# Weight sums in DRAM as half pieces on two queues, and the last product of a layer by block of tokens, in a two-layer streaming encoder

## The chip, the cores and the metric

The kernel runs on one core of one Trainium2 chip. The metric is the device time of one execution in microseconds (us). The core has TensorE (PE) for matmuls, whose results go to banks of PSUM; VectorE (DVE), ScalarE (ACT) and GpSimd (POOL) for elementwise work; and SyncE (SP), which here only issues DMAs. [...] Each engine works through its own instructions in order.

## The reference

One inference step over 1024 prompt tokens and 64 tokens of a running stream, all in float32, model width 1024. Layer 0 is a Mamba-2 (SSD) mixer and a SwiGLU feed-forward network (FFN), layer 1 a chunk-band attention with a learned relative bias and an FFN. Every sub-layer has a norm before and after it:

```python
for layer in range(DEPTH):
    if layer < N_A:            # layer 0
        mp = ssd_mixer(rmsnorm(xp, nw[0]), h0, c0, *params)
    else:                      # layer 1
        kp, vp = shared_kv(xp, kv_norm_w, w_kv)
        mp = prompt_band_attention(rmsnorm(xp, nw[0]) @ attn_w_q, kp, vp, attn_rel_bias) @ attn_w_o
    xp = xp + rmsnorm(mp, nw[1])
    xp = xp + rmsnorm(swiglu(rmsnorm(xp, nw[2]), ffn_w_in[layer], ffn_w_out[layer]), nw[3])

def swiglu(u, w_in, w_out):    # hidden width 2816
    g, up = split(u @ w_in, 2)
    return (silu(g) * up) @ w_out
```

The sample tokens go through the same with their own states and caches; outputs are also the new SSD states, convolution rows and the keys and values.

## The kernel before

Activations lie transposed, features on the 128 partitions and the 1088 tokens along the free axis. Every float32 operand is split into a rounded part (hi, made by ACT) and the rest (lo, by DVE), and each product is three matmuls. Tokens are cut in two ways: three slices `SL` of 384, 384 and 320 tokens (s = 0, 1, 2) for the mixer's and the attention's projections, and four quarters `QS` of 256, 256, 288 and 288 (q = 0 to 3) for the rest; blocks b = 0 (q0, q1, 512 tokens) and b = 1 (q2, q3, 576 tokens) are the halves of the FFN.

PE's order is the order in which the program is written out. The program keeps a model clock (`Stream`): side work (norms, splits, the scan's steps, loads) are generator tasks, which yield `(cost, delay, condition)`; a task goes on when the model clock has passed its delay and its condition holds, and what it issues then stands at that place. `st.wait_for` turns the model clock forward until something is there. The other engines' orders come from a scheduler with priorities (`tc.high_priority`). `Ring` objects count tiles: a task that needs tiles of a full ring waits.

The stages, with the times of the profile:

- *Scan* (to about 650 us). 18 groups of two (the last of three) weight tiles of `w_in`, each applied to slices 0, 1, 2: six products ("units") a group. A product ends in one of two PSUM banks named mm; DVE empties it (L798: zs or craw). Beside it `ssd_task` runs for every head pair and slice: it loads a table row MT broadcast over the partitions from DRAM (L922, on SP's queue), DVE takes the column's part off (L931), ACT exponentiates, and PE multiplies. The convolution on ACT starts at L836.
- *Weight sums* (`weight_sums`, L594 to L617). The FFN's second matrix w_f2 is applied by Winograd's form of a 2x2 block product with seven products P1 to P7 instead of eight. Four of them take sums and differences of the matrix's quarters, made once in DRAM: the tensors wsum of each layer, for eight tiles of rows in four groups of two. Each group has five steps: a copy (L608, SP), a sum onto it (L609, POOL), two copies (L610, SP), a sum (L611, POOL), a sum (L612, POOL). The sums of both layers are issued in the scan, three steps ahead of each group from the fifth on.
- *FFN of layer 0* (`back`): first matrix, plain for six pairs and by seven products for the rest, then the second matrix by seven products in the order P1, P6, P7, P5, P4, P2, P3 (`PROD2`); each for four groups g of output rows with 11 tiles of hidden features in two weight parts. `gate2` (L1636 on) puts the products together. After P4 the quarters q1 and q2 are whole, after P3 q0 and q3.
- *Ends.* For a whole quarter, `end(q)` loads the residual stream (delay `EP_W`), computes the norm with `rb_steps` (a transpose of the sums of squares, nst L522; a chain of small DVE steps that makes the reciprocal root nr, L533 to L546; then, `ER_W` later, a broadcast nbp, L552) and applies it (L1566, L1567). `end_slice(s)` splits slice s of the result for the attention (ACT L1591, DVE L1592), sums its squares and, `EQ_W` later, has the next norm's factor made. Slice 0 needs q0 and q1, slice 1 q1 and q2, slice 2 q2 and q3.
- *Attention* (about 1591 to 2100). For each of eight head pairs j a key, value and query product per slice, nine units a pair; between them score, softmax and value steps per block of 128 queries. It begins with values and keys of slice 1, then of slice 0.
- *Output projection and FFN of layer 1*, where P3 already runs first for block 0 and then for block 1.

Weights go through `Weights`: a load on SP into ring raw, a split into ring hl (ACT L363, DVE L364). A pair of w_f1 tiles also has its sum made by a DMA sum on POOL (`aq` in `advance`, L286).

Of the kernel before, what the change touches and what calls it, by code (L numbers as in the profile page):

```python
# [2 lines left out]

# [10 lines left out]
ALU = mybir.AluOpType  # L14
# [36 lines left out]
TB_W, TB_V = 1.0, 10.0  # L51
ES = 0.5, 0.5, 0.4, 0.0
OS = 1.9, 1.4
EP_W, ER_W, EQ_W = ((1.5, 9.4, 12.0, 1.5), (4.0, 9.4, 12.0, 0.0)), (4.0, 8.9, 8.9, 4.0), (5.0, 8.0)

HIP = 3000
BYP = 0, 0, 800, 800
# [178 lines left out]
class Weights:  # L236
# [38 lines left out]
    def advance(self):  # L275
        moved = True
        while moved:
            moved = False
            while self.tq and self.tt.free():
                it = self.tq.pop(0)  # L280
                it["T"] = self.tt.get()
                self.loaded = self.nc.sync.dma_start(it["T"].rearrange("p (e k) -> p e k", e=2), it["two"][0])
                if self.behind is not None:
                    self.tc.add_manual_dep(self.loaded.ins, self.behind.ins.name, ORDER, reason="place in the order")
                self.aq.append((self.clock() + ACC_W, it))
            while self.aq and self.aq[0][0] <= self.clock():  # L286
                it = self.aq.pop(0)[1]
                self.nc.gpsimd.dma_start(it["T"], it["two"][1], accum_op=ALU.add)
                it["added"] = True
            while self.lq and any(r.free() for r in self.raws):  # L290
                self.load()
            if self.sq and len(self.sq[0]["raw"]) == len(self.sq[0]["src"]):
                it = self.sq[0]
                moved = self.plain(it) if len(it["src"]) == 1 else self.pair(it)
# [105 lines left out]
def hybrid_kernel(  # L400
# [188 lines left out]
            UC.put(c)  # L589


    last_g = [None]

    def weight_sums(layer):  # L594

        w2, z, n = w_f2[layer], wsm_[layer], HF * P

        def sp(x):
            tc.add_manual_dep(x.ins, W.loaded.ins.name, ORDER, reason="place in the order")

        def pool(x):
            tc.add_manual_dep(x.ins, last_g[0].ins.name, ORDER, reason="place in the order")

        steps = []
        for g in range(4):
            a, b, to = w2[2 * g], w2[2 * g + 1], z[:, g]
            steps.append((
                lambda g=g, to=to: sp(nc.sync.dma_start(to[:, 2:4, :], w2[2 * g:2 * g + 2, :, :n].rearrange("e p k -> p e k"))),  # L608
                lambda b=b, to=to: pool(G.dma_start(to[:, 2:4, :], b.rearrange("p (e k) -> p e k", e=2), accum_op=ALU.add, max_dma_last_dim=4 * n)),  # L609
                lambda a=a, to=to: (sp(nc.sync.dma_start(to[:, 0, :], to[:, 3, :])), sp(nc.sync.dma_start(to[:, 1, :], a[:, n:]))),  # L610
                lambda a=a, to=to: pool(G.dma_start(to[:, 0, :], a[:, :n], accum_op=ALU.add)),  # L611
                lambda to=to: pool(G.dma_start(to[:, 1, :], to[:, 0, :], accum_op=ALU.add)),  # L612
            ))
        for f in range(5 + 3):
            for g in range(4):
                if 0 <= f - g < 5:
                    yield steps[g][f - g]  # L617

    order = []
    for g in range(NG):  # L620
# [94 lines left out]
    with ExitStack() as es:  # L715
# [92 lines left out]
        class Conv:  # L808
# [5 lines left out]
            def __call__(self, s, ps_):  # L814
                ct = self.ct
                dst = self.dst[s] = sb2.tile([P, 384], F32, tag=self.tag, bufs=self.bufs, name=self.tag)
                raw = sb2.tile([P, 390], F32, tag="craw", bufs=4, name="craw")
                if s == 0:
                    G.memset(raw[:, 0:3], 0.0)
                else:  # L820
                    G.tensor_copy(raw[:, 0:3], self.prev[:, 0:3])
                if s < 2:
                    w_ = 384
                    scaled(raw[:, 3:387], ps_, s, 0, 384)
                    self.prev = sb2.tile([P, 4], F32, tag="halo", bufs=5, name="halo")
                    last_g[0] = G.tensor_copy(self.prev[:, 0:3], raw[:, 384:387])
                else:
                    w_ = 323
                    G.tensor_copy(raw[:, 259:262], scs[:, ct, :])
                    scaled(raw[:, 3:259], ps_, s, 0, 256)  # L830
                    scaled(raw[:, 262:326], ps_, s, 256, 64)
                    G.tensor_copy(cst[:, ct, 0:3], raw[:, 256:259])
                    G.tensor_copy(cst[:, ct, 3:6], raw[:, 323:326])

                cw = C_CW + ct * 4
                A.activation(dst[:, :w_], raw[:, 0:w_], AF.Identity, bias=col(C_CB + ct), scale=col(cw))  # L836
                for k in range(1, 4):
                    V.scalar_tensor_tensor(
                        dst[:, :w_], raw[:, k:k + w_], col(cw + k), dst[:, :w_], op0=ALU.mult, op1=ALU.add
                    )  # L840
                if s < 2:
                    A.activation(dst[:, :384], dst[:, :384], AF.Silu)
                else:
                    A.activation(dst[:, 0:256], dst[:, :256], AF.Silu)
                    A.activation(dst[:, 256:320], dst[:, 259:323], AF.Silu)
                    A.activation(dst[:, 320:384], ident[:, 0:64], AF.Copy, scale=0.0)
# [307 lines left out]
            pend[s] = [dps] * (s < 2) + box  # L1154
        finish(2)
        side[0] = pyy
        staged = chain_of(weight_sums(0), weight_sums(1))
        for i, grp in enumerate(order):
            for _ in range(3 if i > 3 else 0):
                next(staged, lambda: None)()  # L1160
            ws = [W.get() for _ in grp]
            ev = [evac_of(*f) for f in grp]
            if len(grp) < 3:
                seq = [(i, s) for s in range(NSL) for i in range(len(grp))]
                if grp is order[0]:

                    seq = [(0, 0), (0, 1), (1, 0), (1, 1), (1, 2), (0, 2)]
            else:
                seq = [(0, 0), (1, 0), (0, 1), (0, 2), (2, 0), (1, 1), (2, 1), (1, 2), (2, 2)]
            for i, s in seq:  # L1170
                kd_, jj_ = grp[i]
                q = 3 * jj_ + s
                if kd_ == "x":
                    st.wait_for(lambda: so["C"] > q - 5)
                elif kd_ == "z":
                    st.wait_for(lambda: so["D"] > q - 3)
                elif kd_ == "C" and q >= 5:
                    g_, s_ = divmod(q - 5, 3)
                    st.wait_for(lambda: so["C"] > 3 * (4 * g_ + 3) + s_)
                unit(ws[i], u[s], SL[s][1], lambda p_: ev[i](s, p_))  # L1180
                if s == 2:
                    W.put()
        nc.sync.dma_start(cst_o, cst)
# [141 lines left out]

    SEVEN = (P1, (0, 0), None), (P6, None, 0), (P7, None, 3), (P5, None, 2), (P4, None, 1), (P2, (1, 0), None), (P3, (1, 1), None)

    PROD2 = [[(*x, bs) for x in SEVEN for bs in (((0,), (1,)) if lay and x[0] == P3 else ((0, 1),))] for lay in range(2)]

    ACT2 = {P1: 4, P6: 2, P2: 5, P7: 0, P5: 1, P4: 6, P3: 3}  # L1330

# [89 lines left out]
    def back(layer, start, cpost, xsrc, xmid, cpre, cpost2, xout, rb_out, done2):  # L1421
# [3 lines left out]
        with ExitStack() as es:  # L1425
# [230 lines left out]
            def gate2(p_, g, ps, b):  # L1656
# [24 lines left out]
                if p_ == P2:  # L1681
                    add_sq(ssq[q0], a, n, g == 0)
                elif p_ == P5:
                    add_sq(ssq[q1], d, n, g == 0)
                elif p_ == P4:
                    add_sq(ssq[q1], c, n, False)
                elif p_ == P3 and b and g == 3 and rb_out is None:

                    more[0] = ssum_start(n)
                    A.activation(more[0][:, :n], b_, AF.Square)  # L1690
                elif p_ == P3:
                    add_sq(ssq[q0], b_, n, False)

            for p_, _, _, bs in PROD2[layer]:
                for g in range(4):
# [28 lines left out]
                if p_ in (P4, P3):  # L1724
                    for b in bs:
                        q = ((1, 2) if p_ == P4 else (0, 3))[b]
                        st.spawn(end(q, yq[q], ssq[q], more[0] if q == 3 else None))
                    if rb_out is not None:
                        for s in (1,) if p_ == P4 else (0, 2):
                            st.spawn(end_slice(s))  # L1730
            W.pri = 0
            assert RX.live == 0
# [39 lines left out]
    with ExitStack() as es:  # L1772
# [30 lines left out]
        def load_bias(j):  # L1803

            bias = []
            for e in range(2):
                bt = late["sb3"].tile([P, WIN], F32, tag="bias", bufs=3, name="bias")
                nc.sync.dma_start(bt, bass.AP(rbrow.tensor, (2 * j + e) * 768, [[1, P], [1, WIN]]))
                G.memset(bt[0:64, 0:64], NEG)
                G.memset(bt[64:128, 576:640], NEG)  # L1810
                bias.append(bt)
            kqv[j]["bias"] = bias

        def evk(j):
            d = kqv[j]

            def f(s, p_):
# [8 lines left out]
                        G.memset(Kd[:, T:].bitcast(F32), 0.0)  # L1826
                for e, Kd in enumerate(d["Kt"]):
                    hi, lo = Kd[H2[e], 384 * s:384 * s + n], Kd[H2[1 - e], 384 * s:384 * s + n]
                    A.copy(hi, kf[H2[e], :n])
                    V.tensor_tensor(lo, kf[H2[e], :n], hi, op=ALU.subtract)  # L1830
                d["K"].add(s)
                if s:
# [239 lines left out]
        st.wait_for(lambda: cur["A"] >= 3)  # L2072
        units(wq, 0, evq, (2,))
        W.put()
        for j in range(1, 8):
            if j > 1:
                load_pair(j)
# [9 lines left out]
            while left:  # L2087
# [12 lines left out]
                if (s, i) == (2, 0):  # L2100
                    st.spawn(side_task(j))
                units(ws[i], j, evs[i], (s,))
                if s == 2:
                    W.put()
                if j == 7 and i == 2:
# [153 lines left out]
```

## Time and profile before

| | us |
|---|---|
| median of three runs | 2953.83 (2951.97 to 2958.01) |
| profiled execution, its time | 2944.86 |
| profiled execution, its span | 2943.2 |
| PE busy | 2858.4 |
| DVE busy | 2131.8 |
| ACT busy | 1424.9 |
| POOL busy | 605.3 |

The span runs from the first to the last instruction of the profiled execution. A matmul's busy time is modelled, so a stretch in which PE is busy throughout can still be one in which it runs at a lower clock; the clock that was granted stands beside the busy times. In the lines below, `A <- B` after a wait means that A's engine stood idle until B was done; `DMA x<-y` is the landing of a transfer. A row that begins with a time is one instruction: start, duration, engine, line, operation, tiles.

### The profile page before, as it was taken

The page shows a single profiled execution, that of the slowest core. Times are in us where ns is not written, and L with a number is a line of the kernel's source. Part 1 is how long each engine was busy: PE and PEld are TensorE (multiplying, and loading weights), DVE is VectorE, ACT ScalarE, POOL GpSimd, SP SyncE. Part 2 cuts the span into 40 slices and gives each one's busy share as a digit, 9 for nine tenths or more (in the row PEclk, how much of TensorE's full clock was granted, in tenths as well). Part 3 has the DMA queues.
Part 4 walks back from the last instruction along what each step waited for, and adds up shares of the span by engine and source line. Part 5 has one row for each costly group of instructions (what it writes and reads, how often), then busy time and mean ns, then how long its engine had stood idle before and what let it go on. Part 6 is the DMA issues. An engine that isn't in the chain of part 4 may idle for free. (4 is left out here: it accounts for less than half of the span.)

```text
span 2943.2 us, 58213 instructions
## 1 busy us (share of the span) xinstructions
PE 2858.4 (97%) x22094; PEld 2810.2 (95%) x22094; DVE 2131.8 (72%) x4834; ACT 1424.9 (48%) x2616; POOL 605.3 (21%) x880
## 2 busy tenths in 40 slices
PE   8999998999999999999999899999999999999999
PEld 8998898999998999999998899999999999999998
DVE  7987786886767665676559877877768766567567
ACT  6655545554554333344345556656565333334343
POOL 1334334340220222221022000000031122221011
PEclk9999999999999999999999999999999999999999
DMA  4439677654647656577655222222368555667666
GB/s 137 129 132 240 179 206 205 182 162 140 191 143 195 160 142 161 139 213 224 191 173 164 89 65 89 77 72 76 100 202 230 144 146 151 161 188 222 194 197 193
DMA packets 261673, 471.30 MB, mean 160 GB/s; under 512 B 26256, under 2 KB 162672, under 8 KB 261392
## 3 DMA queue, kind: packets, MB, share of 16 engines
q1 hardware_dynamic: 241584, 400.40, 42.0%
q0 software_dynamic: 19808, 67.19, 13.3%
q8 instruction: 173, 2.83, 0.4%
q14 instruction: 108, 0.88, 0.1%
HBM read 381.90 MB, written 127.26 MB: 173 GB/s over the span
## 5 line engine op out<-in xcount | busy, mean ns | idle before, releaser
L489 PE MATMUL mm<-r,hl 128*128 128x384 f32 (+2 forms) x1704 | 571.4, 335 | 25.2 <-DVE zs L798 12.4
L490 PE MATMUL mm<-r,hl 128*128 128x384 f32 (+2 forms) x1704 | 552.4, 324 | 2.4 <-DVE r L1592 2.4
L491 PE MATMUL mm<-r,hl 128*128 128x384 f32 (+2 forms) x1704 | 552.1, 324 | 1.4 <-DVE hl L364 0.7
L489 PEld LDWEIGHTS mm<-r,hl 128*128 128x128 f32 x1704 | 324.1, 190 | 31.6 <-DVE zs L798 12.6
L1379 PE MATMUL px<-r,hl 128*128 128x288 f32 (+1 forms) x1184 | 348.8, 295 | 0.0
L490 PEld LDWEIGHTS mm<-r,hl 128*128 128x128 f32 x1704 | 324.2, 190 | 3.3 <-DVE r L1592 3.0
L491 PEld LDWEIGHTS mm<-r,hl 128*128 128x128 f32 x1704 | 323.3, 190 | 2.0 <-DVE hl L364 1.1
L1380 PE MATMUL px<-r,hl 128*128 128x288 f32 x1056 | 313.3, 297 | 4.6 <-DVE hl L364 4.5
L1378 PE MATMUL px<-r,hl 128*128 128x288 f32 x1056 | 311.6, 295 | 0.0
L364 DVE TENSOR_TENSOR hl<-raw,hl 128x1024 fp32r<-128x1024 f32 (+2 forms) x171 | 195.1, 1141 | 92.9 <-ACT hl L363 92.3
L1714 PE MATMUL po<-r,hl 128*128 128x288 f32 (+1 forms) x856 | 246.7, 288 | 0.0
L1715 PE MATMUL po<-r,hl 128*128 128x288 f32 (+1 forms) x856 | 246.7, 288 | 0.0
L1716 PE MATMUL po<-r,hl 128*128 128x288 f32 (+1 forms) x856 | 246.6, 288 | 0.0
L1379 PEld LDWEIGHTS px<-r,hl 128*128 128x128 f32 x1184 | 223.7, 189 | 0.0
L363 ACT CAST hl<-raw 128x1024 fp32r<-128x1024 f32 (+2 forms) x171 | 165.7, 970 | 110.2 <-PE po L1716 41.4
L1378 PE MATMUL px<-rx,hl 128*128 128x256 f32 x768 | 213.8, 278 | 1.6 <-DVE u L1393 1.6
L1380 PE MATMUL px<-rx,hl 128*128 128x256 f32 x768 | 213.9, 279 | 0.3 <-DVE hl L364 0.3
L1380 PEld LDWEIGHTS px<-r,hl 128*128 128x128 f32 x1056 | 200.1, 189 | 5.4 <-DVE hl L364 5.3
L1378 PEld LDWEIGHTS px<-r,hl 128*128 128x128 f32 x1056 | 200.2, 190 | 0.0
L1379 PE MATMUL px<-rx,hl 128*128 128x256 f32 x640 | 178.3, 279 | 0.0
L1714 PEld LDWEIGHTS po<-r,hl 128*128 128x128 f32 x856 | 161.5, 189 | 0.0
L1716 PEld LDWEIGHTS po<-r,hl 128*128 128x128 f32 x856 | 160.9, 188 | 0.3 <-DVE hl L364 0.3
(385 smaller groups left out, 8019.2 us busy)
## 6 DMA issues: line engine op xcount, KB each, us to landing
raw<-in_w_f_dram SPq DMA_DIRECT2D x64, 512.0 KB, 4.9
tt<-in_w_f_dram SPq DMA_DIRECT2D x44, 512.0 KB, 4.1
tt<-in_w_f_dram POOLq DMA_DIRECT2D x44, 512.0 KB, 6.6
raw<-in_w_in_dram SPq DMA_DIRECT2D x40, 512.0 KB, 4.4
MT<-ascr SPq DMA_DIRECT2D x48, 384.0 KB, 4.9
raw<-in_w_so_dram SPq DMA_DIRECT2D x32, 512.0 KB, 3.8
r<-hscr SPq DMA_DIRECT2D x56, 288.0 KB, 3.9
wsum<-in_w_f_dram SPq DMA_DIRECT2D x8, 1408.0 KB, 10.1
```

Of the source, the lines that this page charges most:

```text
L363: self.nc.scalar.copy(h, v)
L364: (eng or self.eng or self.nc.vector).tensor_tensor(lo, v, h, op=ALU.subtract)
L489: PE.matmul(ps[:, :n], h_, xh, start=(first and i == 0), stop=False)
L490: PE.matmul(ps[:, :n], h_, xl, start=False, stop=False)
L491: PE.matmul(ps[:, :n], l_, xh, start=False, stop=(last and i == nk - 1))
L1378: PE.matmul(ps, wh, ah[:, k, :], start=(k == 0), stop=False)
L1379: PE.matmul(ps, wh, al[:, k, :], start=False, stop=False)
L1380: PE.matmul(ps, wl, ah[:, k, :], start=False, stop=(k == 3))
L1714: PE.matmul(ps, wh, xh, start=(k0 > 0 and i == ks[0]), stop=False)
L1715: PE.matmul(ps, wh, xl, start=False, stop=False)
L1716: PE.matmul(ps, wl, xh, start=False, stop=(k0 == 0 and i == ks[-1]))
```

## The change

Five edits are in the diff:

1. The steps of a weight sum are cut into half pieces (`c = n // 2` columns): eight pieces a layer, of six steps each. Copies are issued from ACT's stream, behind the last convolution or key copy named so far (`last_a`), sums from POOL's as before. Three pieces are under way at a time, each doing one step in turn.
2. Layer 0's sums are issued in the scan, one step after each product of slices 0 and 1 from the second group on; layer 1's in the attention, one step after each unit from pair 1 on.
3. P3 of layer 0 is done for block 0 and then for block 1, as layer 1's already is; the end of q0 and slice 0 are put in after the first, the end of q3 and slice 2 after the second. Its weights are loaded and split once for each.
4. Delays are other: `EP_W` of layer 0 for q1 and q2, `ER_W` of q1 and q2 in both layers, `EQ_W` of slices 0 and 1. The squares of P3's results get a high priority.
5. The DMA sum of a pair of w_f1 tiles is issued only when a pair is next to be split.

```diff
-EP_W, ER_W, EQ_W = ((1.5, 9.4, 12.0, 1.5), (4.0, 9.4, 12.0, 0.0)), (4.0, 8.9, 8.9, 4.0), (5.0, 8.0)
+EP_W, ER_W, EQ_W = ((1.5, 3.0, 6.0, 1.5), (4.0, 9.4, 12.0, 0.0)), (4.0, 5.0, 5.0, 4.0), (12.0, 12.0)
...
-            while self.aq and self.aq[0][0] <= self.clock():
+            while self.aq and self.aq[0][0] <= self.clock() and 'two' in self.sq[0]:
...
-        steps = []
-        for g in range(4):
-            a, b, to = w2[2 * g], w2[2 * g + 1], z[:, g]
-            steps.append((
-                lambda g=g, to=to: sp(nc.sync.dma_start(to[:, 2:4, :], w2[2 * g:2 * g + 2, :, :n].rearrange("e p k -> p e k"))),
-                lambda b=b, to=to: pool(G.dma_start(to[:, 2:4, :], b.rearrange("p (e k) -> p e k", e=2), accum_op=ALU.add, max_dma_last_dim=4 * n)),
-                lambda a=a, to=to: (sp(nc.sync.dma_start(to[:, 0, :], to[:, 3, :])), sp(nc.sync.dma_start(to[:, 1, :], a[:, n:]))),
-                lambda a=a, to=to: pool(G.dma_start(to[:, 0, :], a[:, :n], accum_op=ALU.add)),
-                lambda to=to: pool(G.dma_start(to[:, 1, :], to[:, 0, :], accum_op=ALU.add)),
-            ))
-        for f in range(5 + 3):
-            for g in range(4):
-                if 0 <= f - g < 5:
-                    yield steps[g][f - g]
+        c = n // 2
+        def copy(to, x):
+            behind(A.dma_start(to, x), last_a)
+        def add(to, x):
+            behind(G.dma_start(to, x, accum_op=ALU.add), last_g)
+        def steps(g, o):
+            a, b, to = w2[2 * g], w2[2 * g + 1], z[:, g, :, o:o + c]
+            yield lambda: copy(to[:, 2:4, :], w2[2 * g:2 * g + 2, :, o:o + c].rearrange("e p k -> p e k"))
+            yield lambda: add(to[:, 2:4, :], b.rearrange("p (e k) -> p e k", e=2)[:, :, o:o + c])
+            yield lambda: copy(to[:, 0, :], to[:, 3, :])
+            yield lambda: copy(to[:, 1, :], a[:, n + o:n + o + c])
+            yield lambda: add(to[:, 0, :], a[:, o:o + c])
+            yield lambda: add(to[:, 1, :], to[:, 0, :])
+        pieces = [steps(g, o) for g in range(4) for o in (0, c)]
+        live = []
+        while pieces or live:
+            while pieces and len(live) < 3:
+                live.append(pieces.pop(0))
+            for p_ in list(live):
+                f = next(p_, None)
+                if f is None:
+                    live.remove(p_)
+                else:
+                    yield f
...
-        staged = chain_of(weight_sums(0), weight_sums(1))
-        for i, grp in enumerate(order):
-            for _ in range(3 if i > 3 else 0):
-                next(staged, lambda: None)()
+        staged = weight_sums(0)
+        for grp in order:
...
                 unit(ws[i], u[s], SL[s][1], lambda p_: ev[i](s, p_))
+                if s < 2 and grp is not order[0]:
+                    next(staged, lambda: None)()
...
-    PROD2 = [[(*x, bs) for x in SEVEN for bs in (((0,), (1,)) if lay and x[0] == P3 else ((0, 1),))] for lay in range(2)]
+    PROD2 = [[(*x, bs) for x in SEVEN for bs in (((0,), (1,)) if x[0] == P3 else ((0, 1),))] for lay in range(2)]
...
                 elif p_ == P3:
-                    add_sq(ssq[q0], b_, n, False)
+                    with tc.high_priority(HIP):
+                        add_sq(ssq[q0], b_, n, False)
...
-                        for s in (1,) if p_ == P4 else (0, 2):
+                        for s in (1,) if p_ == P4 else (0,) if bs == (0,) else (2,):
                             st.spawn(end_slice(s))
...
+        staged = weight_sums(1)
         for j in range(1, 8):
...
                 units(ws[i], j, evs[i], (s,))
+                next(staged, lambda: None)()
```

More of the change, by code (lines that the diff above doesn't have):

```diff
@@ L1 @@
 from contextlib import ExitStack
-from itertools import chain as chain_of
 import concourse.bass as bass
@@ L589, in drop_u @@
             UC.put(c)
-    last_g = [None]
+    last_g, last_a = [None], [None]
     def weight_sums(layer):
         w2, z, n = w_f2[layer], wsm_[layer], HF * P
[L598 to L602, printed above, removed]
-        steps = []
-        for g in range(4):
-            a, b, to = w2[2 * g], w2[2 * g + 1], z[:, g]
-            steps.append((
-                lambda g=g, to=to: sp(nc.sync.dma_start(to[:, 2:4, :], w2[2 * g:2 * g + 2, :, :n].rearrange("e p k -> p e k"))),
-                lambda b=b, to=to: pool(G.dma_start(to[:, 2:4, :], b.rearrange("p (e k) -> p e k", e=2), accum_op=ALU.add, max_dma_last_dim=4 * n)),
-                lambda a=a, to=to: (sp(nc.sync.dma_start(to[:, 0, :], to[:, 3, :])), sp(nc.sync.dma_start(to[:, 1, :], a[:, n:]))),
-                lambda a=a, to=to: pool(G.dma_start(to[:, 0, :], a[:, :n], accum_op=ALU.add)),
-                lambda to=to: pool(G.dma_start(to[:, 1, :], to[:, 0, :], accum_op=ALU.add)),
-            ))
-        for f in range(5 + 3):
-            for g in range(4):
-                if 0 <= f - g < 5:
-                    yield steps[g][f - g]
@@ new lines, in weight_sums, with behind @@
+        c = n // 2
+        def behind(x, last):
+            tc.add_manual_dep(x.ins, last[0].ins.name, ORDER, reason="place in the order")
+        def copy(to, x):
[10 more added lines that the diff above has]
+            yield lambda: add(to[:, 1, :], to[:, 0, :])
@@ L835, in __call__ @@
                 cw = C_CW + ct * 4
-                A.activation(dst[:, :w_], raw[:, 0:w_], AF.Identity, bias=col(C_CB + ct), scale=col(cw))
+                last_a[0] = A.activation(dst[:, :w_], raw[:, 0:w_], AF.Identity, bias=col(C_CB + ct), scale=col(cw))
                 for k in range(1, 4):
@@ L1809, in load_bias @@
                 G.memset(bt[0:64, 0:64], NEG)
-                G.memset(bt[64:128, 576:640], NEG)
+                last_g[0] = G.memset(bt[64:128, 576:640], NEG)
                 bias.append(bt)
@@ L1828, in f @@
                     hi, lo = Kd[H2[e], 384 * s:384 * s + n], Kd[H2[1 - e], 384 * s:384 * s + n]
-                    A.copy(hi, kf[H2[e], :n])
+                    last_a[0] = A.copy(hi, kf[H2[e], :n])
                     V.tensor_tensor(lo, kf[H2[e], :n], hi, op=ALU.subtract)
```

## The prediction

> **What bounds the kernel now.** I read the page first (parts 1 and 2), then the busy time by stage, then who PE waited for inside the two stages that the change touches, and last the landing times of the small transfers there.
>
> ```profile
> span 2943.2 us, 58213 instructions
> PE 2858.4 (97%) x22094; PEld 2810.2 (95%) x22094; DVE 2131.8 (72%) x4834; ACT 1424.9 (48%) x2616; POOL 605.3 (21%) x880
> ```
>
> TensorE is the bound over nearly the whole span, so a change can only win what PE loses: 2943.2 - 2858.4 = 85 us of idle time, and what it runs at a lower clock. Where that lies, by stage (columns: PE, PEld, DVE, ACT, POOL busy, granted clock, DMA share, GB/s):
>
> ```profile
> 100.00:209.00 109.00, 108.80 (x778) 106.04 (x777) 98.87 (x244) 65.45 (x99) 47.51 (x73) 1.00 0.37 119
> 209.00:500.00 291.00, 269.21 (x1874) 259.85 (x1874) 217.93 (x559) 146.97 (x217) 114.34 (x178) 0.99 0.76 207
> 500.00:620.00 120.00, 120.00 (x838) 118.19 (x837) 100.91 (x263) 65.07 (x97) 50.34 (x80) 1.00 0.74 205
> 1500.00:1560.00 60.00, 60.00 (x486) 60.00 (x486) 38.76 (x81) 26.03 (x51) 12.54 (x13) 1.00 0.58 177
> 1560.00:1591.00 31.00, 29.79 (x240) 29.53 (x240) 28.16 (x73) 18.03 (x44) 10.04 (x12) 1.00 0.50 159
> 1591.00:1660.00 69.00, 55.77 (x304) 52.52 (x303) 58.99 (x196) 41.59 (x114) 2.13 (x10) 0.93 0.39 122
> 1660.00:2084.00 424.00, 417.57 (x3355) 402.74 (x3353) 329.46 (x1029) 251.79 (x619) 11.32 (x73) 1.00 0.25 76
> ```
>
> Two stages hold it. In the scan, 209 to 500 us, PE idles 291.00 - 269.21 = 21.8 us and 1% of clock costs 2.7 more: **24.5 us**. Just before, without weight sums, it idles 0.2. At the step from layer 0 to attention, 1591 to 1660, it idles 69 - 55.77 = 13.2 us and runs at 0.93, 0.07 x 55.8 = 3.9: **17.1 us**. The attention, 424 us, has ScalarE at 59%, GpSimd nearly empty and DMA at a quarter.
>
> The scan's waits, PE's and then VectorE's (209 to 500: total, times, longest):
>
> ```profile
> PE mm L489 <- DVE zs L798: 12.2, 7, 7.0
> PE mm L489 <- DVE craw L798: 7.3, 6, 2.6
> DVE MT L931 <- DMA MT<-ascr: 35.4, 12, 9.5
> ```
>
> PE waits for VectorE to empty a product's bank (L798), and VectorE, which works in order, stands before L931 until the row table MT has come from DRAM. The landing of MT, from issue, in the windows 100 to 209, 209 to 500 and 500 to 640:
>
> ```profile
> DMA to landing us min/median/max: 3.6/4.3/4.8
> ...
> DMA to landing us min/median/max: 4.0/6.8/15.0
> ...
> DMA to landing us min/median/max: 3.6/4.6/5.5
> ```
>
> And the worst case, one row per engine, as it happened:
>
> ```profile
> 433.68 0.61 SPq L608 DMA_DIRECT2D wsum<-in_w_f_dram  x1
> 434.38 0.56 SPq L610 DMA_DIRECT2D wsum<-wsum  x1
> 435.00 0.59 SPq L610 DMA_DIRECT2D wsum<-in_w_f_dram  x1
> 444.44 1.17 POOL L609 DMA_DIRECT2D wsum<-in_w_f_dram  x1
> 444.75 1.85 SPq L922 DMA_DIRECT2D MT<-ascr  x2
> 458.93 1.20 DVE L931 TENSOR_SCALAR MT<-MT,nac 128x128 f32<-128x128 f32 x6 [9.53 <-DMA MT<-ascr]
> 460.65 0.64 PE L489 MATMUL mm<-r,hl 128*128 128x320 f32 x1 [7.01 <-DVE zs L798]
> ```
>
> Three sum copies on SP's queue and a sum on POOL's stand about the two MT loads; VectorE waits 9.5 us and PE 7.0. At an equal total rate (205 GB/s, 500 to 620) PE lost nothing, so what hurts is a burst that meets an MT load, not the mean rate.
>
> At the step to attention PE waits (1591 to 1660):
>
> ```profile
> PE nbp L552 <- DVE nr L546: 4.3, 1, 4.3
> PE mm L489 <- DVE vt L1876: 3.9, 1, 3.9
> PE mm L490 <- DVE r L1592: 2.4, 2, 1.6
> PE mm L489 <- DVE kf L1822: 1.2, 1, 1.2
> ```
>
> All four are VectorE being late: it is busy 58.99 of 69 us with the ends of q0 and q3, the splits of slices 0 and 2, and the first keys and values at once.
>
> **The change part by part.**
>
> *Weight sums in the scan.* The sums now run as 1408 KB and 704 KB transfers:
>
> ```profile
> wsum<-in_w_f_dram SPq DMA_DIRECT2D x8, 1408.0 KB, 10.1
> wsum<-wsum SPq DMA_DIRECT2D x8, 704.0 KB, 6.6
> ```
>
> Per group of rows that is 2 x 1408 + 4 x 704 = 5632 KB, per layer 22.5 MB; before, two layers within 209 to 620, 110 GB/s. After, one layer here: 48 steps at four steps a group, 12 of the scan's 18 groups of about 30 us (an estimate: they fill the windows from 100 on to some 650 us), 63 GB/s, each transfer half as large, no three steps at once, and no sum copy on the queue that carries MT, only on ACT's and POOL's. What remains of 24.5 us: nothing, if it is as from 500 to 620; 12, if the loss goes with the bytes. I take 6, nearer to nothing, because the 63 GB/s over the scan's own 119 are below those 205. **Gain 18.5** (12 to 24.5). SP loses its 24 copy issues. ACT gains 3 x 8 = 24 at 0.59 us (the last L610 row, of a like size), 14 us in 360, of which it is free for half (146.97 busy of 291). POOL's sum issues stay 24. ACT is in order, though: behind a copy that waits for a sum to land stand the convolution's activations (rival 3).
>
> *Weight sums in attention.* Another 22.5 MB, 24 ACT issues (14 us) and 24 POOL issues (at most 1.17 us each, the L609 row of twice the size: 28 us), spread over 48 of 59 products, about 345 us: 76 + 65 = 141 GB/s. ACT has 424 - 251.79 = 172 us free and POOL over 400. Behind a POOL sum that waits stand the paddings of queries and values, behind an ACT copy the exponentials and P copies, for which PE waits. Bounds: 0 (the 100 to 209 row: 119 GB/s, idle 0.2) and 12 (what bytes alone leave in the scan). **Cost 3**, nearer to the quiet row as to its rate.
>
> *P3 of layer 0 by block.* PE does the same matmuls in another order. The eight half rows of weights are loaded and split twice:
>
> ```profile
> L364 DVE TENSOR_TENSOR hl<-rx,hl 128x768 fp32r<-128x768 f32 x13 | 12.4, 956 | 16.6 <-ACT hl L363 16.5
> L364 DVE TENSOR_TENSOR hl<-rx,hl 128x640 fp32r<-128x640 f32 x14 | 11.7, 835 | 2.2 <-ACT hl L363 2.2
> L363 ACT CAST hl<-rx 128x768 fp32r<-128x768 f32 x13 | 10.8, 833 | 15.3 <-PE po L1716 12.6 <-issue 2.7
> ```
>
> 4 x 0.96 + 4 x 0.84 = 7.2 us more of VectorE, some 6 of ACT, and 2.8 MB. For it the end of q0 and slice 0 start at half of P3, near 1575, instead of at 1591. They cost VectorE, after 1591 now:
>
> ```profile
> L1566 DVE SCALAR_TENSOR_TENSOR y<-y,pcs,rb 128x256 f32<-128x256 f32 x8 | 3.5, 481 | 0.3 <-ACT rb L555 0.3
> L1567 DVE TENSOR_TENSOR y<-y,r 128x256 f32<-128x256 f32 x8 | 3.2, 420 | 0.0
> L1592 DVE TENSOR_TENSOR r<-y,r 128x256 fp32r<-128x256 f32 x8 | 2.9, 420 | 0.0
> ```
>
> 3.5 + 3.2 + 2.9 = 9.6 us leave the crowded stretch, and with slice 0's squares some 12. But P3's own stretch has only 31 - 28.16 = 2.8 us of VectorE free. Room comes from the shorter waits (EP_W, ER_W): the end of q2 and slice 1 move from there into 1500 to 1560, where 21 us are free. With 7.2 + 12 coming in and 8 to 13 going out (an end and a slice, by the same rows, with their squares), P3 is still overfull by 3 to 8 us; the gates and weight splits go first there, so that much runs on past 1591, where PE has three products on slice 1 to do (72 matmuls, some 10 us at the scan row's 269.21 / 1874 each) before it needs slice 0. Late next: the bcast of slice 0, since EQ_W is now 12 us, and the first value weights, whose turn comes later as P3 eats weights twice as fast. I leave 7 of 17.1: **gain 10** (2 to 15).
>
> *Shorter ER_W (8.9 to 5.0), both layers.* For q2 the root's chain on VectorE is slow, as q1's end runs between its steps:
>
> ```profile
> 1549.25 0.49 PE L522 MATMUL nst<-ident,ssum 128*128 128x128 f32 x3
> 1556.34 0.71 DVE L546 SCALAR_TENSOR_TENSOR nr<-nv 128x3 f32<-128x3 f32 x1
> 1559.37 0.49 PE L552 MATMUL nbp<-ident,nr 128*128 128x128 f32 x3
> ```
>
> From nst to the root's end 7.8 us, to nbp 10.1; 3.9 less is 6.2, so PE would stand 1.6 us. Layer 1 has the same chain with the same wait: as much again. **Cost 3.2** (0, if the earlier place finds VectorE free, to 6, if it finds it twice as late).
>
> *The rest.* The new condition for the second sums of the w_f pairs finds the plain weights already split, since three hl tiles hold them; the last group's pair wait (1.6 us, next row) could move by its own size either way, and I cost it at nothing. The priority of P3's squares reorders 0.4 us pieces on ACT that no PE wait names.
>
> ```profile
> PE px L1378 <- DVE u L1393: 1.6, 1, 1.6
> ```
>
> **Sum.** 18.5 + 10 - 3 - 3.2 = 22. Against the profiled execution (2944.9 us, span 2943.2): 2923. The median of the timed runs is 2953.8, 9 us higher than that execution, so I put it at 2953.8 - 22 = **2932**.
>
> **Rivals.**
> 1. *The queue does not matter, only bytes do.* Then 12 of the scan's loss stay, and attention pays 6: 12.5 + 10 - 6 - 3.2 = 13, 2941. For it: POOL's sums stand about the late MT too, and they stay. Against it: equal rates from 209 to 500 and 500 to 620 with unequal landings. [...]
> 2. *The step to attention is not relieved.* Slice 0 needs room in ring R: of 16 tiles slice 1 holds 6, P3's second block 6 and q0's residual 2, so slice 0 waits for P3's last quarter, and VectorE is overfull. Gain 2 instead of 10: 18.5 + 2 - 3 - 3.2 = 14, 2940.
> 3. *ACT blocks* (slower). One copy of each piece, 16 in all, waits on ACT for a sum to land. On POOL such waits cost now:
>
> ```profile
> POOL wsum L612 <- DMA wsum<-in_w_f_dram: 12.1, 3, 5.5
> POOL wsum L609 <- DMA wsum<-in_w_f_dram: 5.3, 2, 4.3
> ```
>
> About 4 us each when they happen. If PE felt 22 / 16 = 1.4 us of each, nothing would be won; at 2.1 us, 33 us are lost, 11 slower than before: 2965. Against it: a piece's next step comes three products later, 15 us, and transfers of sums land in 6.6 to 10.1 (the rows above).
> 4. *Both gains weak* (1 and 2 together, with some of 3): 2950.
> 5. *Nothing comes back*: 24.5 + 15 = 39, 2915.
>
> **How the numbers follow.** Chances: forecast 0.50 (2922 to 2941 by its own bounds), rival 1 0.15, rival 2 0.12, rival 4 0.08, rival 3 0.08, rival 5 0.07. Within 0.2% (5.9 us, about what a measurement of this kernel can tell from no change) falls rival 4; slower is rival 3; the rest, 0.84, is faster. From 2917 to 2946 leaves out rivals 3 and 4 and half of 5.
>
> **What the profile after would show.** MT landing under 8 us throughout, the L931 wait on MT under 10 us in the scan and PE idle there under 8; the same waits near 18 mean rival 1. After P3, L1592 gone from PE's waits and the clock near 1.00; the waits nr and vt still at 4 mean rival 2. A wait of PE for nr of 1 to 2 us at each q2. ACT's waits for wsum landings near zero; tens of us mean rival 3. New PE idle over 5 us between 1660 and 2084 would make the attention cost wrong.

## The result: slower, because the attention lost more than the scan gained

The changed kernel takes 2967.99 us (median of 7 runs, 2963.68 to 2978.93) against 2951.61 for the kernel before: ratio 1.0069, 95% interval [1.0047, 1.009]. The forecast was 2932, faster. The profiled execution of the changed kernel took 2976.23 us, the second longest of the seven, so sizes read from it lean high; that of the kernel before (2944.86) lies 6.8 us under its median. Below, "before" and "after" are the two kernels. One run of e9_no_sums1 further down (3364.06 us, at a granted clock of 0.777 where its other runs show 0.991 to 0.994) is left out of its median and ratio. The head of after's profile:

```profile
span 2974.5 us, 58336 instructions
PE 2876.8 (97%) x22094; PEld 2828.2 (95%) x22094; DVE 2143.4 (72%) x4842; ACT 1425.4 (48%) x2620; POOL 626.6 (21%) x904
```

PE does the same 22094 matmuls, is busy 18.4 us longer and idles 12.9 us more. To find where, take rows that mark the same work in both traces: the first product of layer 0's second matrix (po, first start) and the score products of the attention (S, first and last start). Before, then after (operation, count, durations in ns, first to last start, shapes):

```profile
L1714 PE MATMUL po<-rx,hl x376: 276/281/369, 1358.9 to 2909.2; 128*128 128x256 f32 x132, 128*128 128x288 f32 x56
L1913 PE MATMUL S<-K,Qh x208: 220/309/499, 1647.1 to 2129.1; 128*128 128x320 f32 x64, 128*128 128x128 f32 x16, 128*128 128x256 f32 x8, 128*128 128x384 f32 x8
```

```profile
L1724 PE MATMUL po<-rx,hl x376: 276/281/377, 1346.9 to 2940.8; 128*128 128x256 f32 x132, 128*128 128x288 f32 x56
L1923 PE MATMUL S<-K,Qh x208: 220/309/637, 1634.1 to 2157.2; 128*128 128x320 f32 x64, 128*128 128x128 f32 x16, 128*128 128x256 f32 x8, 128*128 128x384 f32 x8
```

Up to layer 0's second matrix the change is 12.0 us ahead (1358.9 to 1346.9), at the first score 13.0. Across the attention, first to last score, before takes 482.0 and after 523.1: **41.1 us lost**. What follows adds 3.2. 41.1 + 3.2 - 13.0 = 31.3, the difference of the spans. (Some expectations below count to the end of the last score, 482.3 and 523.4; those of e1_anchor, e2_scan and e4_sp begin later, at the last wait for slice 2's keys, and call the same stretch 447 and 488, some 35 us less.)

The stages of after: the scan in two windows, the step to attention, and the attention from the first score to the last; then the attention of before (columns as in the prediction):

```profile
100.00:209.00 109.00, 105.47 (x757) 102.78 (x754) 89.03 (x237) 59.23 (x88) 46.73 (x71) 0.98 0.63 176
209.00:500.00 291.00, 286.29 (x2000) 279.91 (x1999) 238.89 (x600) 160.91 (x241) 127.40 (x196) 0.99 0.61 158
1584.00:1634.00 50.00, 41.38 (x220) 40.02 (x220) 45.49 (x136) 29.23 (x80) 2.25 (x8) 0.90 0.44 142
1634.00:2158.00 524.00, 489.95 (x3829) 468.43 (x3828) 380.15 (x1175) 290.27 (x712) 34.91 (x103) 0.96 0.43 117
```

```profile
1647.00:2130.00 483.00, 473.16 (x3828) 454.88 (x3827) 378.24 (x1175) 290.99 (x712) 13.31 (x79) 1.00 0.26 79
```

In the attention idle time grew from 9.8 us (483 - 473.16) to 34.1, and the same matmuls took 16.8 us longer (489.95 - 473.16) at a clock of 0.96: 24.2 + 16.8 = 41.0.

### One stall, row by row

How a stall of this kind comes about is told by one boundary between two head pairs in the trace of after (start, duration, engine, line, operation, and in brackets the idle time before it and what ended it):

```profile
1758.14 0.15 POOL L1836 MEMSET K<- 128x64 f32 x1 [45.18 <-PE S L1924]
1762.70 0.14 POOL L1819 MEMSET bias<- 64x64 f32 x1 [3.72 <-DMA bias<-in_rbrow_dram]
1762.90 0.15 POOL L1820 MEMSET bias<- 64x64 f32 x1
1763.17 2.82 POOL L605 DMA_DIRECT2D wsum<-in_w_f_dram  x3
1765.28 1.32 SPq L1801 DMA_DIRECT2D cr<-in_ckT_dram  x2
1773.36 0.48 ACTq L602 DMA_DIRECT2D wsum<-wsum  x1
1773.94 0.51 ACT L1861 CAST Qh<-qf 64x384 fp32r<-64x384 f32 x1 [7.68 <-DMA wsum<-in_w_f_dram]
1774.49 0.55 DVE L1863 TENSOR_TENSOR Ql<-qf,Qh 64x384 fp32r<-64x384 f32 x1 [6.47 <-ACT Qh L1861]
1775.29 0.58 PE L1923 MATMUL S<-K,Qh 128*128 128x256 f32 x1 [4.46 <-DVE pT L1958]
1776.87 0.47 PE L488 MATMUL mm<-r,hl 128*128 128x320 f32 x1
1781.16 0.31 PE L488 MATMUL mm<-r,hl 128*128 128x320 f32 x1
```

- POOL has stood 45.18 us before a padding of the keys (L1836), whose buffer the scores of an earlier pair still read. Then come the paddings of the bias tiles (L1819, L1820).
- The diff makes the second of these, L1820, the instruction behind which a sum is placed (`last_g[0] = G.memset(bt[64:128, 576:640], NEG)`). So sums that the program issued one by one, a product apart, all stand behind paddings that wait for a pair to end, and leave together: three in 2.82 us, with copies on ACT's queue about them. It is the same at every pair: all 24 sums of layer 1 leave within 17 us after one of six such paddings of the keys.
- The loads of the keys' cache (cr, L1801) and the weights go out just behind them, and the DMA engines are full: from 1770 to 1777 the windows show a DMA share of 1.07 and 1.08 and up to 284 GB/s, against 0.43 and 117 over the whole attention. The next copy of a piece (1773.36) waits on ACT for a sum to land, and with it the query's split (7.68 us), DVE (6.47) and PE (4.46).
- PE's next matmuls of 320 columns take 0.47 us instead of 0.31, and start 0.27 us apart instead of 0.145; the granted clock is 1.00 from 1770 to 1774, 0.51 from 1774 to 1781 and 1.00 again from 1781 to 1783. The matmuls are slow for some 5.5 us, so this stall cost more than its 4.46 us of idle time.

The same picture in sums over the attention of after: PE's largest wait (2.1 us in before, so it holds 22.4 of the 24.2 us of new idle time), then ACT's on transfers.

```profile
PE S L1923 <- DVE pT L1958: 24.5, 11, 4.8
...
ACT Ck L1803 <- DMA cr<-in_ckT_dram: 17.4, 7, 5.1
ACT Qh L1861 <- DMA wsum<-in_w_f_dram: 15.7, 2, 8.0
...
ACT sc L1938 <- DMA wsum<-in_w_f_dram: 8.6, 1, 8.6
```

And the wait was there to be read before the change (POOL's waits in the attention of before; L1826 and L1809 are after's L1836 and L1819):

```profile
POOL K L1826 <- PE S L1914: 228.4, 10, 45.2
POOL Qh L1845 <- PE S L1913: 68.9, 8, 12.9
POOL bias L1809 <- DVE mx L1923: 59.8, 4, 49.5
```

Of the "over 400 us free" that the prediction gave POOL, little was so: these three rows alone are 357 of the stage's 483 us. POOL was idle, but standing before instructions that could not run yet.

### The profile page after: what moved, and what is told of

It is laid out like the page before. It is cut to its first block, busy times and chain, and to the rows that moved or that the text cites. A ratio compares the mean times of both kernels' runs of the same rounds, so it can differ in the third digit from the quotient of the medians.

```text
span 2974.5 us, 58336 instructions
## 1 busy us (share of the span) xinstructions
PE 2876.8 (97%) x22094; PEld 2828.2 (95%) x22094; DVE 2143.4 (72%) x4842; ACT 1425.4 (48%) x2620; POOL 626.6 (21%) x904
## 5 line engine op out<-in xcount | busy, mean ns | idle before, releaser
L1416 POOL TENSOR_TENSOR u<-u,c 128x256 f32<-128x256 f32 (+1 forms) x76 | 60.9, 802 | 487.1 <-DVE u L1414 404.0
L1724 PEld LDWEIGHTS po<-r,hl 128*128 128x128 f32 x856 | 162.3, 190 | 0.0
```

The source lines that it names most:

```text
L1416: G.tensor_tensor(x["u3"], x["u3"], x["c22"], op=ALU.mult)
L1724: PE.matmul(ps, wh, xh, start=(k0 > 0 and i == ks[0]), stop=False)
```

## The experiments

Three theories for the attention: the sums bunch because of the instruction they are placed behind ("the anchor", theory A), or ACT is held by its own copies, wherever the sums stand (B), or the bytes and issues of the sums cost it as such (C). Further: what in the scan was worth what, and what P3 by block is worth.

**e1_anchor.** One edit to the changed kernel:

```diff
-                last_g[0] = G.memset(bt[64:128, 576:640], NEG)
+                G.memset(bt[64:128, 576:640], NEG)
```

> Edit: the padding of the bias tiles no longer sets the place that POOL's sums must stand behind; everything else is the changed kernel. The attention lasts 447 us before and 488 after (from the last short wait for slice 2's keys to the last score of pair 7). Theory A (POOL works in order, its sums stand behind paddings that wait for a buffer until a pair is done, then go out in a bunch beside the cache loads of the next pair): the sums are spread, the attention falls to 455 to 470. Theory B (an ACT copy that waits for a sum to land holds ACT, wherever the sums stand): 475 to 488. Theory C (the bytes and the issue time of the sums in the attention cost it): 485 to 490.

Measured: 2934.17 us, ratio 0.9956 [0.9942, 0.9971]. Scores and ACT's wait on the cache in the attention; no row of ACT names a sum's landing any more:

```profile
L1923 PE MATMUL S<-K,Qh x208: 220/309/582, 1625.3 to 2114.5; 128*128 128x320 f32 x64, 128*128 128x128 f32 x16, 128*128 128x256 f32 x8, 128*128 128x384 f32 x8
ACT Ck L1803 <- DMA cr<-in_ckT_dram: 7.2, 5, 4.8
```

And POOL at the corresponding place, where the sums now leave one or two at a time, 3.6 to 15 us apart:

```profile
1718.08 0.83 POOL L605 DMA_DIRECT2D wsum<-in_w_f_dram  x1 [14.51 <-DMA wsum<-wsum]
1732.93 1.81 POOL L605 DMA_DIRECT2D wsum<-in_w_f_dram  x2 [14.02 <-DMA wsum<-wsum]
1736.57 0.81 POOL L605 DMA_DIRECT2D wsum<-wsum  x1 [1.84 <-DMA wsum<-in_w_f_dram]
```

The attention takes 489.2 us instead of 523.1, 33.9 less; the ratios of the two kernels to the one before differ by 0.0113, about 33 us. Theory A asked for 455 to 470 in its own measure, which is 490 to 505 here, so the result is just under its lower end; B and C asked for 510 or more. One assignment in one line decided the sign of the whole change, with the same bytes and the same copies: the anchor's theory holds.

**e4_sp.** The changed kernel, anchor and all, with layer 1's copies on SP's queue instead of ACT's:

```diff
-            behind(A.dma_start(to, x), last_a)
+            if layer:
+                tc.add_manual_dep(nc.sync.dma_start(to, x).ins, W.loaded.ins.name, ORDER, reason="place in the order")
+            else:
+                behind(A.dma_start(to, x), last_a)
```

> Edit: the copies of layer 1's sums in the attention go from SP's stream instead of ACT's; sums stay where they are on POOL; the rest is the changed kernel. Theory B: ACT waits for no sum any more, the attention falls from 488 to 465 or less. Theory A: the bunches stay, ACT still waits for the cache loads, 470 to 488, with the waits for wsum now on SP, where other loads stand behind them. Theory C: 485 to 490.

Measured: 2961.26 us, ratio 1.0051 [1.0036, 1.0067]. Scores, and ACT's wait on the cache:

```profile
L1926 PE MATMUL S<-K,Qh x208: 221/309/686, 1629.1 to 2140.6; 128*128 128x320 f32 x64, 128*128 128x128 f32 x16, 128*128 128x256 f32 x8, 128*128 128x384 f32 x8
ACT Ck L1806 <- DMA cr<-in_ckT_dram: 23.3, 11, 5.3
```

511.5 us, as theory A asks (B asked for 500 or less). With ACT freed of its copies 11.6 of the 41 come back; the other 29.5 stay while the sums go out in bunches, and ACT's wait moves to the cache's rows, which land late (6.3 us at the median, 2.7 in before). The two numbers are no clean shares, because SP now stands before the copies as ACT did: it waits 10.6 us for sums to land, and loads stand behind these copies. Holding ACT is a part of the loss, not its source; how large a part stays open.

**e9_no_sums1.** The changed kernel without layer 1's 24 sums (its last products then work with weights that lack them); its copies stay on ACT:

```diff
-            behind(G.dma_start(to, x, accum_op=ALU.add), last_g)
+            if not layer:
+                behind(G.dma_start(to, x, accum_op=ALU.add), last_g)
```

> As the changed kernel, but layer 1's 24 accumulating transfers (the sums, GpSimd's) are left out and the 24 copies on ScalarE's queue stay at their places, so layer 1's last products use wrong weights. Theory 'the sums released together at a pair's end cost attention its time, the copies only pass it on': attention (first to last score matmul) 482 to 488 us instead of 523.4, no wait of ScalarE for a sum's landing, span 2930 to 2940. Rival 'the 24 copies and their 17 MB on ScalarE's queue cost a good part by themselves': over 495 us.

Measured: 2926.72 us (median of three), ratio 0.9932 [0.9915, 0.995]; the profiled span, 2923.5, lies under the 2930 to 2940 expected.

```profile
L1924 PE MATMUL S<-K,Qh x208: 220/309/496, 1624.2 to 2107.3; 128*128 128x320 f32 x64, 128*128 128x128 f32 x16, 128*128 128x256 f32 x8, 128*128 128x384 f32 x8
```

483.1 us, 1.1 more than before: the copies (8 of 704 KB and 16 of 352 KB, 11.3 MB and not the 17 of the expectation) cost the attention next to nothing when they have no sum to wait for. With e1_anchor (489.2), sums that are spread cost about 6, sums that are bunched 40.

**e1c_spread.** As e1_anchor, with the paddings of bias and keys placed behind the last sum, so that none runs ahead:

```diff
-                last_g[0] = G.memset(bt[64:128, 576:640], NEG)
+                late_set(bt[64:128, 576:640], NEG)     # placed behind the last sum issued
...
-                        G.memset(Kd[:, T:].bitcast(F32), 0.0)
+                        late_set(Kd[:, T:].bitcast(F32), 0.0)
```

> As e1_anchor, but the bias and key paddings on GpSimd are placed behind the last sum issued, so that no sum can run far ahead of its product. Theory 'bunching is gone with the anchor': attention (first to last score matmul) 487 to 492 us as in e1_anchor (489.5), ratio 0.994 to 0.997. Rival 'what is left over before (7 us) is still sums going out together': attention 483 to 486, ratio 0.992 to 0.9945. If the paddings now hold up the pair's first scores, attention is over 495.

Measured: 2937.72 us, ratio 0.9959 [0.9942, 0.9975]; scores from 1627.4 to 2115.4, 488.0. No more to be had there; what the remaining 6 us of the sums are made of stays open.

**e2_scan.** The changed kernel with both layers' sums in the scan, as half pieces on the two queues, one step after every product:

```diff
-        staged = weight_sums(0)
+        staged = chain_of(weight_sums(0), weight_sums(1))
...
-                if s < 2 and grp is not order[0]:
+                if grp is not order[0]:
```

> Edit: layer 1's sums go to the scan as well, behind layer 0's, one step after each product from the second group on; no sums in the attention; the rest is the changed kernel. All theories: the attention is back at 447 us. The scan tells how much of its gain was the halved bytes and how much the half pieces and the other queue: PE idle there was 22 us before and is 8 after. If the bytes count, it is 20 or more again and the kernel ends 5 to 8 us below before for nothing but other effects; if pieces and queues count, 8 to 12, and the kernel ends 10 us below before.

Measured: 2954.18 us, ratio 1.0034 [1.0017, 1.0052]. Its scan by stage, and PE's waits from 100 to 640:

```profile
100.00:209.00 109.00, 100.50 (x723) 98.01 (x723) 86.37 (x229) 54.58 (x82) 51.47 (x75) 0.97 0.69 186
209.00:500.00 291.00, 281.10 (x1961) 273.76 (x1960) 233.41 (x582) 155.55 (x235) 130.83 (x200) 0.99 0.73 189
500.00:640.00 140.00, 132.42 (x915) 129.02 (x915) 111.68 (x279) 70.81 (x109) 56.16 (x92) 0.99 0.68 178
```

```profile
PE mm L489 <- DVE craw L808: 14.5, 8, 8.3
PE mm L489 <- DVE zs L808: 9.3, 6, 3.8
```

It idles 8.5 + 9.9 + 7.6 = 26.0 us in these windows; before idled 0.2 + 21.8 + 0. Smaller pieces and other queues brought nothing back: the loss was spread over the scan, not lowered. The idle time is what the case of the bytes asks. The time is not: both cases put the kernel 5 to 10 us under the one before, and it came out 8 above. A marker of the whole scan, the transposes of xsT (tile xtp) from the first to the last, says the same: 575.7 us here, 569.7 in before, 569.3 in e3_p3, which has before's sums. The attention takes 485.1, 3.1 more than before.

**e7_spqueue.** As e1_anchor, with layer 0's copies on SP's queue, which carries the MT loads (the edit of e4_sp with `not layer` for `layer`).

> As e1_anchor, but layer 0's copies of the scan go out on SP's queue, which carries the MT loads, instead of ACT's; bytes, pieces and places are the same. Prediction's case 'a copy ahead of MT in its own queue is what hurts': MT lands later (over 10 us at worst), scan idle rises from 10 to 14 to 20 us, ratio 0.997 to 1.000. Rival 1 'only bytes matter': scan idle stays at 9 to 12 us, ratio 0.994 to 0.9975, as e1_anchor.

Measured: 2940.43 us, ratio 0.9976 [0.9965, 0.9987]. PE's waits from 100 to 640 in it, and then in e6_sums_only, which ran beside it with the copies on ACT's queue:

```profile
PE mm L488 <- DVE zs L810: 10.0, 4, 5.0
PE mm L488 <- DVE craw L810: 1.9, 2, 1.3
```

```profile
PE mm L488 <- DVE zs L807: 7.3, 4, 2.6
PE mm L488 <- DVE craw L807: 2.6, 2, 1.8
```

11.9 us of waiting against 9.9, within the 9 to 12 that rival 1 asks; the slowest MT took 11.9 us to land, against 8.0, and this is what the prediction's case asks (over 10), as is the ratio. The whole scan, by the transposes of xsT, takes 559.9 us. The eight kernels that share its sums, pieces and places but have the copies on ACT's queue (after, e1_anchor, e1c_spread, e4_sp, e5_waits, e6_sums_only, e6_again, e9_no_sums1) take 552.8 to 556.1. So the queue is worth about 4 to 7 us in this one trace. Part of it is idle time, 12.4 us in the windows from 100 to 640 against 8 to 11 in the eight; from 100 to 209 the clock is lower as well, 0.97 against 0.98 to 1.00. The interval of e5_waits [0.9945, 0.9973], an ACT-queue kernel too, overlaps with that of e7_spqueue, so the times alone would not show it. In e2_scan the other queues brought nothing back, so what these 4 to 7 us come from stays open.

**e3_p3.** The kernel before with P3 of layer 0 by block, the other delays and the priority of the squares, and nothing else of the change:

```diff
-EP_W, ER_W, EQ_W = ((1.5, 9.4, 12.0, 1.5), (4.0, 9.4, 12.0, 0.0)), (4.0, 8.9, 8.9, 4.0), (5.0, 8.0)
+EP_W, ER_W, EQ_W = ((1.5, 3.0, 6.0, 1.5), (4.0, 9.4, 12.0, 0.0)), (4.0, 5.0, 5.0, 4.0), (12.0, 12.0)
...
-... in (((0,), (1,)) if lay and x[0] == P3 else ((0, 1),))] for lay in range(2)]
+... in (((0,), (1,)) if x[0] == P3 else ((0, 1),))] for lay in range(2)]
```

> Edit: the kernel before with P3 of layer 0 by block and the other delays alone (weight sums as before, on SP, both layers in the scan). If the loss of the change is the attention's, this one is within 4 us of before: P3 takes 39 us instead of 35, as the root of q0 is asked for before POOL has added its squares, and the stretch from P3's end to the keys of slice 2 takes 60 instead of 66. If the step to attention is what failed most, it is 8 us or more slower.

Measured: 2947.66 us, ratio 1.0001 [0.9988, 1.0014]. PE's waits from 1560 to the first score, at 1641:

```profile
PE nbp L552 <- DVE r L1592: 4.7, 1, 4.7
PE mm L491 <- DVE hl L377: 3.1, 1, 3.1
PE nst L522 <- POOL ssq L515: 1.9, 1, 1.9
PE nst L522 <- POOL ssum L515: 0.9, 1, 0.9
```

10.6 us, where before waited 11.8 (4.3 + 3.9 + 2.4 + 1.2) from 1591 on. The product's waits for vt and r went and others of the same size came: a weight split (hl L377), the broadcast (nbp, still, now behind r of L1592), and a root asked for before its squares were there (nst). With everything counted from 1560 to the first score, idle time went from 12.9 to 11.4 us and the granted clock from 0.94 to 0.98. From the start of layer 0's second matrix to the first score it takes 283.5 us against 288.2 before, 4.7 less; the attention then takes 2.8 more (484.8) and layer 1's P2 1.3 more. P3 took 37.9 us where 39 was expected.

**e6_sums_only.** As e1_anchor, with P3, ends, slices and delays as before.

> As e1_anchor, but P3 of layer 0, its ends, slices and waits are as before: the sums alone with the freed anchor. Theory 'by block is worth nothing' (e3_p3: -8 after P3, +2.9 in P3, +2.8 in attention, +1.3 in layer 1): the whole saving of e1_anchor is the scan's 12, minus 2 to 4 in attention; ratio 0.9945 to 0.997, within 3 us of e1_anchor. Rival 'by block is worth its 10 us' (the prediction): 6 to 10 us slower than e1_anchor, ratio 0.998 to 0.9995.

Measured: 2932.45 us, ratio 0.9946 [0.9931, 0.996]; against e1_anchor's 0.9956 that is no difference: P3 by block is worth nothing here. The traces show why the sum is nil: from the second matrix to the first score the eight kernels with P3 by block and the changed delays take 283.4 to 287.2 us and the four without 287.5 to 288.8, some 3.5 less; with spread sums the attention then takes 488.0 to 489.2 instead of 485.4 to 487.6, and layer 1's P2 1.3 more. The same kernel again, as a measure for e8_even:

> The same kernel as e6_sums_only, as the measure for e8_even on the same chip: ratio 0.993 to 0.996.

Measured: 2935.0 us, ratio 0.9959 [0.9945, 0.9972].

**e5_waits.** As e1_anchor, with longer delays where its rows show PE standing:

```diff
-EP_W, ER_W, EQ_W = ((1.5, 3.0, 6.0, 1.5), (4.0, 9.4, 12.0, 0.0)), (4.0, 5.0, 5.0, 4.0), (12.0, 12.0)
+EP_W, ER_W, EQ_W = ((4.0, 3.0, 6.0, 3.0), (4.0, 9.4, 12.0, 0.0)), (4.0, 5.0, 8.9, 4.0), (6.0, 12.0)
```

> As e1_anchor, but the waits of the ends and slices in layer 0 are longer where its records show PE standing before them (EP_W 1.5 to 4 and 3, ER_W of q2 back to 8.9, EQ_W of slice 0 from 12 to 6). Theory 'shorter waits brought VectorE forward too early': layer 1's P2 comes back from 34.8 to 33.5 us, layer 0's P3 from 37.7 to about 35.5, ratio to before 0.993 to 0.995 (2927 to 2931). Rival 'VectorE is simply full there, the waits only choose the place': P2 of layer 1 returns, but P3 and the stretch after it lose as much elsewhere, ratio 0.995 to 0.997 as e1_anchor.

Measured: 2935.9 us, ratio 0.9959 [0.9945, 0.9973]. PE's waits from 1540 to 1634:

```profile
PE mm L490 <- DVE hl L376: 5.0, 2, 4.8
PE nbp L551 <- DVE r L1601: 4.3, 1, 4.3
PE nst L521 <- DVE ssum L1608: 3.0, 1, 3.0
PE mm L488 <- DVE vt L1886: 0.9, 1, 0.9
```

Layer 1's P2 came back (34.8 to 33.8 us), but P3 took 40.2 us, where e1_anchor took 37.7 and the theory asked for 35.5. My idea that the shorter delays were at fault fell: 13.2 us of waits stand here as well, with other names. The delays choose which of VectorE's pieces is late, as the rival said.

**e8_even.** As e6_sums_only, with the 48 steps of layer 0 over 16 groups instead of 12:

```diff
-                if s < 2 and grp is not order[0]:
+                if (s == 0 or (s, i) == (1, 0)) and grp is not order[0]:
```

> As e6_sums_only, but layer 0's 48 steps go out three to a group of scan products instead of four, over 16 groups (to about 640 us) instead of 12 (to about 500). Theory 'what the scan still loses (9.9 us in e6_sums_only, between 100 and 500) goes with the rate of the sums there': rate down by a quarter and the quiet end filled, idle 5 to 8 us, ratio 1 to 2 per mil below e6_sums_only in the same comparison. Rival 'same bytes, same loss, only at another place': idle 9 to 11, the two within 1 per mil.

Measured: 2929.6 us, ratio 0.9946 [0.9931, 0.996], beside e6_again's 0.9959 [0.9945, 0.9972]. The scan's idle time went from 10.3 to 7.3 us, as a loss that follows the rate would have it, but the scan as a whole takes 553.1 us, within the 552.8 to 556.1 of the eight kernels named under e7_spqueue; in the time the two can't be told apart either. This, e6_sums_only and e1_anchor are the fastest complete kernels here, 0.4 to 0.5% under the kernel before, and none is clearly ahead of the others.

## Why the prediction was wrong, step by step

- **Weight sums in attention, "Cost 3"**: this step failed, with 41 us in the profiled execution. It costed issues and bytes: ACT's free time, POOL's free time, a DMA rate near that of a quiet row. The bytes were no more than it reckoned with (117 GB/s, where it took 141, and the quiet row has 119). What failed is "POOL over 400" us free: POOL was standing for most of it, and the sums stood behind what it waited for. The step even wrote that "behind a POOL sum that waits stand the paddings", and looked only at that direction; what counted is which padding a sum stands behind and what that one waits for (e1_anchor, e9_no_sums1). With the sums spread the attention takes 485.3 to 489.2 in the complete kernels, against 482.0: a cost of 3.3 to 7.2, within the bounds of 0 to 12 that it gave.
- **Rival 3** (ACT blocks on copies) gave 2965, near the 2968 measured, but by another way; that is luck. ACT did wait 24.3 us for sums' landings (15.7 + 8.6). Its counter-argument, a step comes 15 us later and a sum lands in 6.6 to 10.1, assumed that a sum is issued at its step; here sums stood behind paddings before which POOL waited up to 49.8 us, and transfers of wsum landed in up to 15.1. And in e4_sp, without copies on ACT, 29.5 of the 41 stayed.
- **Weight sums in the scan, "Gain 18.5"**: a gain, mis-sized. At the start of layer 0's second matrix after is 12.0 ahead; the scan itself, by the transposes of xsT, takes 556.1 instead of 569.7 us, 13.6 less, and over the eight kernels named under e7_spqueue the gain is 13 to 17. In the window that the prediction reckoned in, 209 to 500, the residue in after is 4.7 idle and about 2.9 of clock, close to the 6 taken. Missed was the window ahead of it: the sums now begin at the second group, and 100 to 209 loses 3.5 us idle and 2.1 of clock (105.47 busy at 0.98), where it lost 0.2. Of the reason given, that the copies must leave MT's queue, e7_spqueue supports a part, 4 to 7 us; the larger part is **rival 1**'s, the bytes (e2_scan). Its price fits too: 12 were to stay, 13.2 did.
- **P3 by block, "gain 10"**: failed; 1.0 in the profiled execution (288.2 to 287.2 us from the second matrix to the first score), some 3.5 over all traces, given back later, and nothing in the time (e3_p3, e6_sums_only). **Rival 2** had this outcome, with a gain of 2; no run tests its reason, room in ring R. The prediction saw that VectorE is overfull, named what would be late next, and then still took 10. The products no longer wait for L1592, but the broadcast nbp does (4.7 us in after too, where the line is L1601), and the clock from 1584 to 1634 is 0.90, not near 1.00. The waits for nr and vt went; the sum of the waits stayed.
- **Shorter ER_W, "Cost 3.2"**: right in kind, less than half in size. Layer 1's P2 takes 34.8 us instead of 33.5 in after, e1_anchor and e7_spqueue, and 33.5 again in e6_sums_only. In after PE stands 0.7 us before nbp there, not 1.6. Layer 0's P2 shows no such wait (33.5 to 33.8, with three broadcasts more in it). Cost 1.3.
- **The rest at nothing**: no row of PE's waits names the pair's condition; the squares are named by the nst waits alone, 2.8 us in after and in e3_p3.
- **What the profile after would show**: MT landing "under 8 us throughout" was just missed, 8.3. VectorE's wait on MT from 209 to 500 fell from 35.4 to 8.1 us and PE's idle time there to 4.7, as forecast; with 100 to 209 included they are 16.3 and 8.2. ACT's waits for wsum came to tens of us, the sign of rival 3, and PE's new idle time between 1660 and 2084 was far over 5, the sign that the attention cost is wrong.

By the terms: -12.0 (up to the second matrix) - 1.0 (step) + 41.1 (attention) + 3.2 (layer 1 and the rest) = +31.3 in the profiled executions, where -22 was predicted. In the medians the change is some 16 to 20 us slower.

## What to carry to other kernels

Before work is put on an engine that looks idle, read what its instructions wait for: an in-order engine that stands 45 us before one padding has no free time for what is queued behind it, and work issued evenly comes out in bunches. The instruction behind which a transfer is placed is as much a part of a change as the transfer; ask when that instruction can run. Where VectorE was full here, delays and orders only chose which wait appeared, so sum the waits of the stage before crediting the one that will go.

## What the runs showed of the hardware

Sums released together slowed small loads on another queue here. Landing times in the attention, in us from issue: cache loads (cr, SP's queue) before, in after, in e1_anchor.

```profile
DMA to landing us min/median/max: 2.4/2.7/5.8
```

```profile
DMA to landing us min/median/max: 4.8/7.9/9.0
```

```profile
DMA to landing us min/median/max: 2.4/4.5/8.1
```

With the same bytes in after and e1_anchor, the median is 7.9 against 4.5: here it counted when transfers met, and the mean rate (117 and 125 GB/s) did not show it. The transfers of wsum, copies included, landed in 3.3 to 15.1 us in after and 3.3 to 11.6 in e1_anchor; the sums of 704 KB took 12.7 us at the median in after and 9.2 in e1_anchor.
